# Two more output tiles by seven products behind an attention stage, and less plain work per run of it

## The chip, the cores and the metric

One core of a Trainium2 chip runs the kernel. TensorE multiplies, VectorE (DVE in the profile), ScalarE (ACT) and GpSimd (POOL) work on tiles, SyncE (SP) issues nearly all DMAs from one queue. The metric is the device time of one execution in microseconds (us). Before the change it is 987.44 us, the median of three runs (986.08 to 991.76).

## The reference, cut to what matters

One layer of neighbourhood attention over 2048 tokens (a grid of 32 rows and 64 columns), 1024 channels, 16 heads of 64 channels; all in float32.

```python
h = rmsnorm(x, g)
q, k, v, gate = split(h @ w_in, 4)                # 2048x1024 @ 1024x4096
# each query sees 8 rows x 16 columns of keys; rpb is a bias per head and offset
p = softmax(where(col_valid, q k^T / 8 + bias, -1e30))
x = x + ((p v) * silu(gate)) @ w_out              # 2048x1024 @ 1024x1024
return rmsnorm(x, norm_f)
```

## The kernel before, in words

A float32 product is taken as three TensorE matmuls: each operand is split into a high part (ScalarE, a copy to the fp32r type) and the rest (VectorE, a subtraction), and high x high, high x low and low x high are added up in PSUM. A pair of output tiles can be had in two ways. The plain way takes for each of four 128x512 quarters eight blocks of the inner dimension, 4 x 24 = 96 matmuls of 128x512. The other way is a scheme of seven products on sums and differences of the quarters (`order7`, `uses`), 7 x 12 = 84 matmuls, with more additions on VectorE and ScalarE.

Stage one and stage two compute the projections, mostly by seven products, and store q, k, v and the gate to DRAM. Six half projections of the last head pairs are left over: 288 plain matmuls. Then comes the attention stage, a loop of 32 *runs* over `order`. One run is one head pair p and one quarter T of the token rows. Run m does, in program order:

- `begin(m)` queues loads for the runs to come on SP (gate, bias tables `em`, q, k, v), each with a mark of TensorE that it must wait for (`not_until`);
- `feed` hands out plain products, some `amount[m]` of them, with `normalise` of the run before and splits of weights (`consume`, `split_rows`) between them;
- `turns(m-1)` transposes the attention weights of the run before (`ph`, 48 transposes) and ScalarE and VectorE copy them to SBUF (`pta`);
- `scores(2m)`, `scores(2m+1)`: 64 matmuls into `s`; VectorE adds the bias table, takes the extreme and writes `sums`; ScalarE takes the exponential into `x` with its sum; VectorE takes reciprocals; POOL normalises six of the eight tiles `x`, VectorE and ScalarE one each;
- `values(m-1)`: 36 matmuls into `o`, times the gate on VectorE, and a store to DRAM.

So plain products stand on TensorE between the value products and the next transposes, while the other engines turn scores into weights. The plain products are those 288, and then the first `PLAIN` output tiles (48 matmuls each, `outputs`). All other output tiles follow behind the attention stage by seven products (`rows_by_seven`, tiles in pairs from `PAIRS`). `amount` sets how many plain products each run gets: `dense` for the first runs, the rest spread evenly. In run 0 the loop also splits two input tiles (`consume(2, turn=True)`).

A bias table is of a kind: `top` for T = 0, `mid` for T = 1 and 2, `end` for T = 3. Run m brings the table of its kind; T = 0 also uses the `mid` of T = 1, T = 3 that of T = 2. Before, `order` takes T = 1 and 0 of all eight head pairs, then T = 2 and 3 of all; so each pair's `mid` is loaded twice.

Of the kernel before, what the change touches and what calls it, by code (L numbers as in the profile page):

```python
# [11 lines left out]
F32 = mybir.dt.float32  # L12
# [12 lines left out]
NP = H // 2  # L25
# [6 lines left out]
RES_BUFS, RES_EARLY = 3, 1  # L32
PLAIN = 4
BUSY = 2
# [28 lines left out]
def build(ctx, tc, x, xr, xt, wg, bias, w_out, n0, nf, out):  # L63
# [20 lines left out]
    raw = pool("raw", 6)  # L84
    kp = pool("kp", 1)
# [1112 lines left out]
    def projections():  # L1198
        for n, (kind, j, ph, c) in enumerate(halves):
            state["half"] = n  # L1200
            w = (KINDS[kind] + j, ph)
            for a in range(2):
                if n == len(halves) - 5 and a == 0:
                    for k in range(RES_EARLY):
                        load_res(*turns_[k])
                if n == len(halves) - 1:
                    if a == 0:
                        store(("ogl",), 20, lambda: load_og(0))
                        store(("ogl",), 38, lambda: load_og(1))
                    else:  # L1210
                        store(("og0",), 13, lambda: split_og(0))
# [22 lines left out]
    def load_k(p, T, part=None, at="values"):  # L1234
# [55 lines left out]

    def load_bias(p, T):
        fs = []
        kind = BRINGS[T]
        w = 2 * WIDE * TABLES[kind][2]
        EM[p, T // 2, kind] = []
        for quad in range(2):
            t = mp([128, 512], F32, "em")[:, :w]
            EM[p, T // 2, kind].append([t[:, :w // 2], t[:, w // 2:]])
            o = TABLE_AT[kind] + quad * w
# [34 lines left out]
    def scores(i, between=None):  # L1334
# [18 lines left out]
        for half, (u, n) in enumerate(HALF_ROWS[T]):  # L1353
            table = EM[p, T // 2, kinds_of[T][half]][quad]
            rows = [t[:, :24 * n].rearrange("p (r c) -> p r c", c=24) for t in sums[2 * half:2 * half + 2]]
# [124 lines left out]
    def add_rows(n, j, ps):  # L1480
        xr = RES.pop((n, j))
        state["event"] = clock[0]
        if n not in Y:
            Y[n] = [None, None], tiny.tile([128, 8], F32, name="st3")
        y, st = (raw if j and n < 1 else ev)([128, 512], F32, "y"), Y[n][1]
        Y[n][0][j] = y
# [88 lines left out]

    turns_ = [(0, 0), (1, 0), (2, 0), (0, 1), (1, 1), (2, 1), (3, 0), (3, 1)]
    place = {}
# [217 lines left out]
    cycles = len(order)  # L1795
    dense, end_of_it = 13.5, 24
    amount = [dense] * 25
    first = 16
# [3 lines left out]
    HALF_HEAD, HEAD = 2, 5  # L1802
    amount += [(96 * (12 - len(units_two)) + 48 * PLAIN - sum(amount) - first - end_of_it) / (cycles - 25)] * (cycles - 25) + [end_of_it - 6]
    fill = projections()
# [31 lines left out]
    def begin(m):  # L1836
# [118 lines left out]
```

## Time and profile before

| | us |
|---|---|
| median of 3 runs | 987.44 |
| the profiled execution | 987.61 |
| its span, first to last instruction | 985.8 |
| stages ahead of attention | 0 to 561.6 |
| attention, 32 runs | 561.6 to 865 |
| products behind attention | 865 to 979.5 |
| tail | 979.5 to 985.8 |

The granted clock of TensorE is 0.998 over the span. Busy times are those of the hardware profiler; matmuls are pipelined, so that a busy TensorE alone doesn't say how fast it goes, and the distance between starts is what counts.

### The profile page before, as it was taken

Reading aid. Unit: us, or ns where it says so; the run is one execution under the profiler, and the core shown is the slowest. Engines: PE = TensorE matmul, PEld = TensorE weight load, DVE = VectorE, ACT = ScalarE, POOL = GpSimd, SP = SyncE. Lnnn points to the kernel's source line nnn. Section 1 sums busy time; section 2 is a strip of 40 time slices with the busy share of each in tenths; the row PEclk is TensorE's granted clock in tenths of the full one; section 3 lists DMA queues with packets and bytes.
Section 4 is the critical chain, followed back from the end, with each engine's and each line's share of the span. In section 5 each row is a group of like instructions: output and inputs, shape, how many; then the busy total and the mean of one; then the engine's idle time right before and its main releaser. Section 6 shows DMA issues by size and latency. Waiting matters only on the chain.

```text
span 985.8 us, 22680 instructions
## 1 busy us (share of the span) xinstructions
PE 977.6 (99%) x8172; PEld 795.1 (81%) x8172; DVE 755.4 (77%) x1735; ACT 531.4 (54%) x1310; POOL 154.4 (16%) x378
## 2 busy tenths in 40 slices
PE   9999999999999999999999999999999999999997
PEld 6888888888888888888888777777777778788886
DVE  5899888988565876766776577677778888877866
ACT  7873245365535342333433377777777777653443
POOL 0000001222100000000001043333332333311110
PEclk9999999999999999999999999999999999999999
DMA  8943647777957846657555799888988988796854
GB/s 281 341 129 107 197 126 255 245 236 253 371 157 226 269 135 177 203 174 226 185 174 184 238 306 294 258 253 255 305 288 273 289 237 264 241 383 181 212 141 117
DMA packets 151617, 226.37 MB, mean 230 GB/s; under 512 B 13776, under 2 KB 67152, under 8 KB 151504
## 3 DMA queue, kind: packets, MB, share of 16 engines
q1 hardware_dynamic: 148480, 219.80, 70.6%
q0 software_dynamic: 2592, 4.72, 2.9%
q8 instruction: 65, 1.06, 0.4%
q14 instruction: 48, 0.39, 0.1%
q10 hardware_dynamic: 432, 0.40, 0.1%
HBM read 158.80 MB, written 66.06 MB: 228 GB/s over the span
## 4 chain that ended last, share of the span: by engine, by line
PE 98%; DMA 1%; SPq 0%; ACT 0%; issue 0%; DVE 0%
PE pp L447 41%; PE pv L613 13%; PE py L1725 12%; PE o L1423 8%; PE s L1347 6%; PE ph L1398 5%; PE pp L389 2%; PE pp L385 2%; PE pp L387 2%; PE pv L728 2%; PE po L1630 2%; PE po L1634 2%; PE po L1632 2%; DMA land<-in_xt_dram 1%; SPq L558 0%
## 5 line engine op out<-in xcount | busy, mean ns | idle before, releaser
L447 PE MATMUL pp<-h,f 128*128 128x512 f32 x576 | 185.3, 389 | 0.0
L447 PE MATMUL pp<-t,f 128*128 128x512 f32 x702 | 171.3, 389 | 0.0
L447 PEld LDWEIGHTS pp<-t,f 128*128 128x128 f32 x702 | 131.8, 188 | 27.4
L1366 ACT ACTIVATE x<-sums,st 128x264 f32<-128x264 f32 (+1 forms) x256 | 124.5, 488 | 29.9 <-DVE st L1358 29.9
L447 PEld LDWEIGHTS pp<-h,f 128*128 128x128 f32 x576 | 108.1, 188 | 22.6
L447 PE MATMUL pp<-l,f 128*128 128x512 f32 x288 | 112.0, 389 | 0.0
L1378 POOL TENSOR_SCALAR x<-x,st 128x264 f32<-128x264 f32 (+1 forms) x192 | 88.6, 477 | 130.1 <-DVE st L1373 106.0
L1358 DVE CUSTOM_DVE_ANT_0 sums<-s,em 128x253 f32<-128x253 f32 (+1 forms) x256 | 91.1, 401 | 5.8 <-ACT x L1366 1.5
L430 DVE TENSOR_TENSOR f<-raw,f 128x512 fp32r<-128x512 f32 x105 | 75.8, 727 | 19.3 <-ACT f L429 19.2
L1423 PEld LDWEIGHTS o<-pta,vt 120*64 120x64 f32 (+2 forms) x1152 | 70.0, 137 | 18.4 <-issue 11.7
L1423 PE MATMUL o<-pta,vt 120*64 120x192 f32 (+8 forms) x1152 | 84.1, 299 | 0.1
L429 ACT ACTIVATE f<-raw 128x512 fp32r<-128x512 f32 x105 | 63.5, 622 | 36.4 <-DVE raw L436 22.0
L1403 DVE COPY pta<-ph 120x512 f32<-120x512 f32 (+2 forms) x96 | 60.3, 682 | 14.8 <-PE ph L1398 14.5
L1405 ACT ACTIVATE pta<-ph 120x512 f32<-120x512 f32 (+2 forms) x96 | 50.3, 595 | 34.2 <-PE ph L1398 34.0
L447 PEld LDWEIGHTS pp<-l,f 128*128 128x128 f32 x288 | 54.1, 188 | 11.2
L1347 PE MATMUL s<-kt,q 64*32 64x253 f32 (+1 forms) x2048 | 59.3, 362 | 0.5 <-issue 0.5
L613 PE MATMUL pv<-wh,t 128*128 128x512 f32 x176 | 56.2, 389 | 0.0
L1725 PE MATMUL py<-woh,f 128*128 128x512 f32 x168 | 55.4, 390 | 0.0
L1398 PEld LDWEIGHTS ph<-ident,x 64*120 64x120 f32 (+2 forms) x1536 | 46.2, 128 | 11.3 <-issue 10.6
L468 POOL TENSOR_TENSOR tmp<-tmp,rb 128x512 f32<-128x512 f32 x18 | 28.5, 1582 | 157.8 <-DVE tmp L465 140.2
L447 PE MATMUL pp<-sixths,f 128*128 128x512 f32 x198 | 52.7, 389 | 0.0
L429 ACT ACTIVATE f<-s 128x512 fp32r<-128x512 f32 x42 | 26.2, 624 | 45.7 <-DVE s L436 39.8
(231 smaller groups left out, 1908.0 us busy)
## 6 DMA issues: line engine op xcount, KB each, us to landing
raw<-in_wg_dram SPq DMA_DIRECT2D x124, 256.0 KB, 5.0
row<-in_xr_dram SPq DMA_DIRECT2D x32, 256.0 KB, 5.1
vd<-v SPq DMA_DIRECT2D x32, 256.0 KB, 3.2
sgd<-sg SPq DMA_DIRECT2D x32, 256.0 KB, 3.3
q<-qd SPq DMA_DIRECT2D x32, 256.0 KB, 4.0
sgt<-sgd SPq DMA_DIRECT2D x32, 256.0 KB, 4.5
ogd<-og SPq DMA_DIRECT2D x32, 256.0 KB, 5.1
em<-in_bias_dram SPq DMA_DIRECT2D x32, 253.0 KB, 4.5
```

The source lines that it names most:

```text
L429: nc.scalar.activation(t[:, 0], src, AF.Copy)
L430: nc.vector.tensor_tensor(t[:, 1], src, t[:, 0].bitcast(F32), OP.subtract)
L447: nc.tensor.matmul(B[n, P], t[:, int(m == 2), c], x[k][int(m == 1)], start=P in (1, 6, 5) and k == 0 and m == 0, stop=k == 3 and m == 2, s ...
L613: nc.tensor.matmul(p, a[:, o], b, start=P in (1, 6, 5) and k == 0 and m == 0, stop=k == 3 and m == 2, skip_group_check=True)
L1347: product = nc.tensor.matmul(places[half, s][h * 32:h * 32 + 32], qt[a, g * 64 + half * 32:g * 64 + half * 32 + 32], kt[a, o:o + n * GW].r ...
L1358: nc.vector.tensor_tensor_reduce(rows[s][:, :, :WIDE], places[half, s].rearrange("p (r c) -> p r c", c=WIDE), table[s].rearrange("p (r c) ...
L1366: nc.scalar.activation(to, rows[s].rearrange("p r (b c) -> p b r c", b=3), AF.Exp, bias=st[:, o:o + 1], scale=-1.0, accum_out=st[:, 4 + o: ...
L1378: nc.gpsimd.tensor_scalar(t, t, f, 1.0, op0=OP.mult, op1=OP.mult)
L1398: one_turn = nc.tensor.transpose(ph[h][:k, o:o + 64], X[quad, half, s][q, at:at + k], ident[q, q])
L1403: nc.vector.tensor_copy(o, i_)
L1423: product = nc.tensor.matmul(o[s * 64:s * 64 + 64, g0 * 64:g1 * 64], vt[:k, strip, s * 64:s * 64 + 64], moving, start=strip == 0, stop=str ...
L1725: nc.tensor.matmul(B[m, P], t[:, a, c], b, start=P in (1, 6, 5) and k == 0 and i == 0, stop=k == 3 and i == 2, skip_group_check=True)
```

## The change

`PLAIN` goes from 4 to 2: two output tiles fewer stand in the attention stage as plain products (96 matmuls), and `PAIRS` has seven pairs instead of six (84 more matmuls behind it). `amount` is 9.7 products for the first 13 runs and the even rest after them, where it was 13.5. For the first three head pairs `order` now takes T = 1, 0, 2, 3 one after the other, and these four runs share one `mid` table of each quad; one of the next pair's two `mid` tables is loaded a run earlier. The two k buffers take turns by load and no longer by pair. Four output half tiles (`turns_`) are left in the stage instead of eight, all in the `ev` buffers, and three lags of their loads and splits are longer.

```diff
-PLAIN = 4
+PLAIN = 2
+SHARED = 3
...
-    order = [(p, T) for p in range(NP) for T in (1, 0)] + [(p, T) for p in range(NP - 2) for T in (2, 3)]
+    order = [(p, T) for p in range(SHARED) for T in (1, 0, 2, 3)]
+    order += [(p, T) for p in range(SHARED, NP) for T in (1, 0)] + [(p, T) for p in range(SHARED, NP - 2) for T in (2, 3)]
...
-                KT[p, T // 2] = (kp([128, 2048], F32, "kt") if p % 2 == 0 else mkp([128, 1536], F32, "kt"))[:, :1344]
+                KT[p, T // 2] = (mkp([128, 1536], F32, "kt") if len(KT) % 2 else kp([128, 2048], F32, "kt"))[:, :1344]
...
+    def table_at(p, T, kind):
+        return p, 0 if p < SHARED else T // 2, kind
+
-    def load_bias(p, T):
+    def load_bias(p, T, upto=2):
...
-        EM[p, T // 2, kind] = []
-        for quad in range(2):
+        got = EM.setdefault(table_at(p, T, kind), [])
+        for quad in range(len(got), upto):
...
-    turns_ = [(0, 0), (1, 0), (2, 0), (0, 1), (1, 1), (2, 1), (3, 0), (3, 1)]
+    turns_ = [(0, 0), (1, 0), (0, 1), (1, 1)]
...
-    dense, end_of_it = 13.5, 24
-    amount = [dense] * 25
+    dense, end_of_it = 9.7, 24
+    many = 13
+    amount = [dense] * many
...
+            if order[m][0] < SHARED and order[m][1] == 2:
+                fs += load_bias(*order[m + 2], 1)
```

What it moves is seen in the order of each engine's instructions. On TensorE, the plain products (`pp`) of run 4 up to its first transpose (`ph`); before, the last eleven of 13:

```order
L387 MATMUL pp<-l,w 128x512
L389 MATMUL pp<-h,w 128x512
L385 MATMUL pp<-h,w 128x512
L387 MATMUL pp<-l,w 128x512
L389 MATMUL pp<-h,w 128x512
L385 MATMUL pp<-h,w 128x512
L387 MATMUL pp<-l,w 128x512
L389 MATMUL pp<-h,w 128x512
L385 MATMUL pp<-h,w 128x512
L387 MATMUL pp<-l,w 128x512
L389 MATMUL pp<-h,w 128x512
L1398 MATMUL ph_6135<-ident,x_5191 120x64
```

and now all of them, from the last value product (`o`) on:

```order
L1428 MATMUL o<-pta,vt 64x128 x2
L388 MATMUL pp<-l,w 128x512
L390 MATMUL pp<-h,w 128x512
L386 MATMUL pp<-h,w 128x512
L388 MATMUL pp<-l,w 128x512
L390 MATMUL pp<-h,w 128x512
L386 MATMUL pp<-h,w 128x512
L388 MATMUL pp<-l,w 128x512
L1403 MATMUL ph_6093<-ident,x_5191 120x64
```

Seven products stand there where 13 stood. By run, from 0 to 31, they are now 39, 10, 9, 13, 7, 9, 10, 10, 12, 7, 10, 10, 11, 11, 11, 12, 10, 14, 8, 14, 8, 11, 11, 11, 11, 12, 11, 13, 10, 10, 14 and 15; before they were 47, 11, 13, 14, 13, 14, 13, 16, 11 and then 13 to 16.

On ScalarE, run 0 between the last exponential and the copies of the transposes; `h` are the two input tiles, `x_5207` the tile that it normalises, `w` weights, `k` a projection on its way out. Before:

```order
L1366 ACTIVATE x_5207,st<-sums,st 128x3x88
L545 ACTIVATE h<-raw 128x512 x2
L371 ACTIVATE k<-pp 128x512
L1380 ACTIVATE x_5207<-x_5207,st 128x3x88
L186 ACTIVATE w<-raw 128x512 x2
L371 ACTIVATE k<-pp 128x512
L1405 ACTIVATE pta<-ph_5388 120x2x4x64
```

Now:

```order
L1371 ACTIVATE x_5207,st<-sums,st 128x3x88
L546 ACTIVATE h<-raw 128x512 x2
L1385 ACTIVATE x_5207<-x_5207,st 128x3x88
L187 ACTIVATE w<-raw 128x512
L372 ACTIVATE k<-pp 128x512
L187 ACTIVATE w<-raw 128x512
L1410 ACTIVATE pta<-ph_5370 120x2x4x64
```

The first `k` has left the run, the second stands between the two weights; VectorE's order in run 0 is the same in both kernels.

On VectorE, run 27 from the gate product (`og`) to the first copy. Before, with an output half tile's addition (`y<-po,xr`) and two scalings:

```order
L1429 TENSOR_TENSOR og<-o,sgt 128x512
L1373 RECIPROCAL st<-st 128x2
L1504 TENSOR_TENSOR y<-po,xr 128x512
L1373 RECIPROCAL st<-st 128x2
L1382 TENSOR_SCALAR x_5205<-x_5205,st 128x3x64
L1546 SCALAR_TENSOR_TENSOR y<-y,st_9124,acc_175 128x512
L1546 SCALAR_TENSOR_TENSOR y<-y,st_9124,acc_176 128x512
L1403 COPY pta<-ph_10469 96x2x4x64
```

Now, with two splits of w_out (`wol`):

```order
L1434 TENSOR_TENSOR og<-o,sgt 128x512
L1378 RECIPROCAL st<-st 128x2 x2
L1387 TENSOR_SCALAR x_5205<-x_5205,st 128x3x64
L193 TENSOR_TENSOR wol<-raw,woh 128x512 x2
L1408 COPY pta<-ph_10308 96x2x4x64
```

The splits of w_out stood in runs 11 to 15 and 19 to 24 before, and stand in runs 16 to 19 and 25 to 29 now; the splits of an output tile's rows (`gl`, two operations each) stood in runs 17, 19, 20 and 25, and stand in 24 and 25.

More of the change, by code (lines that the diff above doesn't have):

```diff
@@ L1207, in projections @@
                     if a == 0:
-                        store(("ogl",), 20, lambda: load_og(0))
-                        store(("ogl",), 38, lambda: load_og(1))
+                        store(("ogl",), 29, lambda: load_og(0))
+                        store(("ogl",), 42, lambda: load_og(1))
                     else:
-                        store(("og0",), 13, lambda: split_og(0))
+                        store(("og0",), 20, lambda: split_og(0))
                 consume(1)
@@ L1353, in scores @@
         for half, (u, n) in enumerate(HALF_ROWS[T]):
-            table = EM[p, T // 2, kinds_of[T][half]][quad]
+            table = EM[table_at(p, T, kinds_of[T][half])][quad]
             rows = [t[:, :24 * n].rearrange("p (r c) -> p r c", c=24) for t in sums[2 * half:2 * half + 2]]
@@ L1484, in add_rows @@
             Y[n] = [None, None], tiny.tile([128, 8], F32, name="st3")
-        y, st = (raw if j and n < 1 else ev)([128, 512], F32, "y"), Y[n][1]
+        y, st = ev([128, 512], F32, "y"), Y[n][1]
         Y[n][0][j] = y
@@ L1802, in build @@
     HALF_HEAD, HEAD = 2, 5
-    amount += [(96 * (12 - len(units_two)) + 48 * PLAIN - sum(amount) - first - end_of_it) / (cycles - 25)] * (cycles - 25) + [end_of_it - 6]
+    amount += [(96 * (12 - len(units_two)) + 48 * PLAIN - sum(amount) - first - end_of_it) / (cycles - many)] * (cycles - many) + [end_of_it - 6]
     fill = projections()
```

2 lines of the change are left out of this document (1 added, 1 removed).

## The prediction, as put on record before the result

> **What bounds the kernel now.** I read the profile page's busy line and its chain first, to see which engine sets the end; then the busy times by stage; then the chain within the attention stage, run by run (run m is pass m of the attention loop, counted from 0).
>
> ```profile
> span 985.8 us, 22680 instructions
> ...
> PE 977.6 (99%) x8172; PEld 795.1 (81%) x8172; DVE 755.4 (77%) x1735; ACT 531.4 (54%) x1310; POOL 154.4 (16%) x378
> ...
> PE 98%; DMA 1%; SPq 0%; ACT 0%; issue 0%; DVE 0%
> ```
>
> TensorE (PE) is 98% of the chain that ended last. So time is saved only by taking matmuls out, and lost only where another engine makes TensorE wait. The stages, one row each (run 0; runs 1 to 12; 13 to 18; 19 to 28; 29 to 31; the products behind attention and the tail):
>
> ```profile
> 561.60:576.40 14.80, 14.80 (x161) 11.14 (x160) 10.37 (x32) 10.14 (x28) 4.53 (x11) 1.00 0.91 298
> 576.40:686.30 109.90, 109.39 (x1938) 86.55 (x1935) 82.83 (x313) 81.67 (x259) 40.99 (x145) 1.00 0.89 267
> 686.30:741.00 54.70, 54.70 (x973) 43.48 (x969) 43.66 (x160) 41.85 (x132) 20.10 (x68) 1.00 0.95 300
> 741.00:833.00 92.00, 91.95 (x1621) 72.91 (x1617) 78.14 (x288) 70.61 (x225) 30.43 (x85) 1.00 0.87 261
> 833.00:865.00 32.00, 32.00 (x534) 25.53 (x531) 27.54 (x95) 22.01 (x71) 9.14 (x22) 1.00 0.80 257
> 865.00:985.80 120.80, 114.50 (x504) 94.40 (x504) 88.32 (x173) 49.94 (x119) 15.89 (x18) 0.98 0.70 205
> ```
>
> After the stage's length come PE, PEld, DVE (VectorE), ACT (ScalarE) and POOL, then the granted clock, the DMA share and GB/s. TensorE is full everywhere; VectorE is at 75% in runs 1 to 12 and 85% in runs 19 to 28 (78.14 of 92.00), with the DMAs at 0.80 to 0.95. The attention stage is where the change takes TensorE work away, so there the other engines' room decides.
>
> **The change, part by part.** First the matmuls. The chain in order of time gives their price:
>
> ```profile
> 695.46 1.87 PE s L1347 x64
> ...
> 699.88 0.43 PE pp L389
> 700.31 0.24 PE pp L385
> ...
> 702.86 0.23 PE pp L389
> 703.09 1.56 PE ph L1398 x48
> 704.65 1.64 PE s L1347 x64
> ...
> 864.96 114.56 PE py L1725 x504
> ```
>
> Behind attention a 128x512 product costs 114.56 / 504 = 0.227 us. In run 14 the 13 plain products between the value products (o) and the transposes (ph) take 703.09 - 699.88 = 3.21 us, one slow first one and then 0.23 each. The change removes two output tiles of 2 x 24 plain products: 96 x 0.23 = 22.1 us. It adds one pair by seven products, 7 x 12 = 84: 84 x 0.227 = 19.1 us. **Term 1: -3.0 us** (at 0.227 for both, -2.7).
>
> Next the cover. A run keeps 9.7 products where it had 13.5, later about 11. Scores go out at the start of a run; VectorE reduces them, ScalarE takes the exponentials, POOL, ScalarE and VectorE normalise, and only then may the transposes come. Run 14 again, in the timeline:
>
> ```profile
> 694.64 1.88 DVE L1403 COPY pta<-ph 88x512 f32<-88x512 f32 x3 [0.20 <-PE ph L1398]
> ...
> 696.57 0.42 DVE L1358 CUSTOM_DVE_ANT_0 sums<-s,em 128x253 f32<-128x253 f32 x1
> ...
> 697.09 0.52 ACT L1366 ACTIVATE x<-sums,st 128x264 f32<-128x264 f32 x1 [0.92 <-DVE st L1358]
> ...
> 701.42 0.52 ACT L1380 ACTIVATE x<-x,st 128x264 f32<-128x264 f32 x1 [0.23 <-DVE st L1373]
> ...
> 701.50 0.47 DVE L1382 TENSOR_SCALAR x<-x,st 128x264 f32<-128x264 f32 x1
> ```
>
> The last normalised tile is ready at 701.97; the transposes start at 703.09 and need it with the 13th of 48, at 703.09 + 13 x 1.56 / 48 = 703.5. Slack: 1.5 us, or 6.5 products. The order of the changed kernel leaves 7 products in runs 4 and 9, 8 in 18 and 20, 9 to 15 elsewhere. Even the shortest, 6 x 0.23 = 1.4 us less than run 14, still fits, by 0.1 us. So the nominal run is covered to its end, with nothing over for anything late. Three places have something late.
>
> *Run 0.* VectorE and ScalarE also normalise and split input tiles there:
>
> ```profile
> 569.08 0.73 DVE L541 SCALAR_TENSOR_TENSOR raw<-raw,g,rb 128x512 f32<-128x512 f32 x1
> ...
> 572.96 0.69 DVE L546 TENSOR_TENSOR l<-raw,h 128x512 fp32r<-128x512 f32 x1 [0.76 <-ACT h L545]
> 573.57 0.22 DVE L1373 RECIPROCAL st<-st 128x2 f32<-128x2 f32 x2
> ...
> 573.89 1.05 POOL L1378 TENSOR_SCALAR x<-x,st 128x264 f32<-128x264 f32 x2 [2.89 <-DVE st L1373]
> ```
>
> and in the chain the transposes that follow:
>
> ```profile
> 574.90 1.56 PE ph L1398 x48
> ```
>
> The reciprocals that POOL needs stand behind those input tiles on VectorE, until 573.79; POOL is done at 574.94. The 11th transpose, which reads POOL's last tile, came at 574.90 + 10 x 1.56 / 48 = 575.22: 0.3 us of slack. VectorE's order up to there is unchanged and its waits are for ScalarE, not for TensorE, so POOL will still end near 574.9. But 8 products go (47 to 39), 1.8 us. **Term 2: 1.8 - 0.3 = +1.5 us**, bounds 0 (the VectorE chain moves forward too) and 1.8.
>
> That wait holds all of TensorE. [...]
>
> *Runs 1 to 6.* Each splits one weight on VectorE between the last normalisation and the copies, as before, after a late start out of run 0. VectorE needs 701.97 - 696.57 = 5.4 us from first reduction to last normalisation and 1.88 for the copies, 7.3 together; every second run has four short reductions, 0.07 us cheaper each, so 7.15 is the mean. A split costs 0.65 and waits for ScalarE:
>
> ```profile
> L1358 DVE CUSTOM_DVE_ANT_0 sums<-s,em 128x253 f32<-128x253 f32 x192 | 73.1, 418 | 5.1 <-ACT x L1366 1.5 <-PE s L1347 0.4
> ...
> L1358 DVE CUSTOM_DVE_ANT_0 sums<-s,em 128x184 f32<-128x184 f32 x64 | 20.4, 347 | 0.7
> ```
>
> ```profile
> 693.15 1.29 DVE L192 TENSOR_TENSOR wol<-raw,woh 128x512 fp32r<-128x512 f32 x2 [0.63 <-ACT woh L191]
> ```
>
> With 0.63 for that wait a run needs 7.15 + 0.65 + 0.63 = 8.4 us of VectorE's time. On TensorE a run is 704.65 - 695.46 = 9.19 us at 13 products, so 6.2 us fixed; six runs with 58 products are 6 x 6.2 + 58 x 0.23 = 50.5 us against 50.4. Balanced: the lag out of run 0 doesn't heal. (Runs 16 to 19, with two w_out splits each and 46 products, come to 36.3 against 35.4; the next paragraph shows that this sum reads high by as much, so nothing is taken for them.) **Term 3: +0.5 us**, bounds 0 and 1.2.
>
> *Runs 25 to 29.* By the changed order the w_out splits, one output tile's split and two additions fall together: 12 VectorE operations in five runs with 56 products. VectorE: 5 x 7.15 + 12 x 0.65 + 5 x 0.63 = 46.7 us; TensorE: 5 x 6.2 + 56 x 0.23 = 43.9. Before, runs 19 to 25 had 18 such operations, between these two starts of scores:
>
> ```profile
> 741.09 1.64 PE s L1347 x64
> ...
> 805.53 1.87 PE s L1347 x64
> ```
>
> The same sum there gives 7 x 7.15 + 18 x 0.65 + 7 x 0.63 = 66.2 us where 64.4 were measured, so it reads 1.3 us too high per five runs. Left: 2.8 - 1.3 = 1.5, of which the transposes' own slack at 10 to 13 products (0.8 to 1.5 us) takes some once. **Term 4: +1.0 us**, bounds 0 and 2.8.
>
> *Table sharing.* Six loads fall away:
>
> ```profile
> em<-in_bias_dram SPq DMA_DIRECT2D x32, 253.0 KB, 4.5
> ```
>
> That is 1.5 MB of the stage's 82 MB (lengths times GB/s above). A load takes 4.5 us and is asked for a run or more ahead, so none is waited for now and none saves time; it offsets what the shorter runs ask for. Were that cover gone, the price is rival D. *Behind attention* VectorE has the roots and scaling of two tiles to do at once, about 2.9 us more (1.7 for the eight small operations from 867.64, 1.42 for two scalings, less 0.2 of overlap), ahead of row sums that had slack:
>
> ```profile
> 867.64 0.21 DVE L1531 TENSOR_SCALAR st<-st 128x1 f32<-128x1 f32 x1
> ...
> 869.35 1.42 DVE L1546 SCALAR_TENSOR_TENSOR y<-y,st,acc 128x512 f32<-128x512 f32 x2
> ...
> 873.40 0.69 DVE L1698 TENSOR_TENSOR s<-raw 128x512 f32<-128x512 f32 x1 [2.63 <-DMA raw<-ogd]
> ...
> 875.59 0.69 DVE L1692 TENSOR_TENSOR f<-s,f 128x512 fp32r<-128x512 f32 x1
> ```
>
> VectorE waited 2.63 us there for a DMA, and the form made at 875.59 is used by the seventh group, at 864.96 + 72 x 0.227 = 881.3. Nothing is paid.
>
> Sum: -3.0 + 1.5 + 0.5 + 1.0 = 0.0 us on the profiled 987.61 (span 985.8 and 1.8 around it), which lies 0.2 over the median of 987.44. **Forecast: 987.4 us, no change.** Bounds: -3.0 gives 984.4, -3.0 + 1.8 + 1.2 + 2.8 = +2.8 gives 990.2. What a measurement can tell from no change is about 0.5%, 4.9 us; no sum of these terms reaches it.
>
> **The rivals.** *B, the cover holds everywhere:* terms 3 and 4 vanish, term 2 partly: 984.4 to 986. For it: VectorE waits 14.5 us in the stage for transposes, time that shorter runs take first (the row under C); against it: run 0's 0.3 us. Price taken: 985.
>
> *C, VectorE becomes the bound of the whole stage (slower):*
>
> ```profile
> DVE pta L1403 <- PE ph L1398: 14.5, 21, 2.6
> ```
>
> The stage's five rows sum to 303.4 us with 242.5 busy on VectorE, 61 idle. About 11 us go with the two tiles (4 additions at 0.69, 4 scalings at 0.71, 4 splits at 0.65, the roots). TensorE's stage becomes 303 - 22 = 281. If VectorE's idle time shrinks only by half of what it waits for transposes (the row above), it needs 231.5 + 61 - 7 = 285.5, +4; if not at all, +11. With -3.0 and run 0's 1.5 that makes 990 to 997; I price it 994. It decides once the average run needs over 8.5 us of VectorE; runs 1 to 6 stand at 8.4.
>
> *D, loads or code come late.* The stage asks for some 4 MB less (tables 1.5, two tiles' attention rows 1.0, their x rows 1.0), 79 MB in 281 us, 280 GB/s against 272: hardly more. But run 10 shows a stall that no semaphore explains:
>
> ```profile
> 657.90 1.85 PE s L1347 x61
> 659.75 0.51 issue
> 660.27 0.61 PE s L1347 x3
> ```
>
> The block of scores took 660.88 - 657.90 = 3.0 us instead of 1.9, with the DMAs at 0.89. One such in every fourth run is 8 us: 993. Against it: one in 32 now.
>
> [...]
>
> **How the numbers follow.** Forecast 0.52, B 0.26, C 0.14, D 0.08. The forecast and most of B lie within 0.5% (982.5 to 992.4); a few hundredths of B could go below, if a stall like run 10's falls away with it; C and D are mostly above, a quarter of them within. Faster 0.04, same 0.78, slower 0.18. The range takes the bounds, 984.4 to 990.2, and a little of C: 984.2 to 991.5.
>
> **What would show it.** Term 1: 588 products at 0.227 behind attention (133.6 us), and TensorE still over 98% of the chain. Term 2: transposes of run 0 waiting for POOL over 1 us. Terms 3 and 4: waits of transposes for VectorE's or ScalarE's normalisation in runs 1 to 6 and 25 to 29, none in 7 to 15. I am wrong if run 0 doesn't wait, if waits stand in every run (C), or if "issue" grows in the chain (D).

## The result, and the profile after

The changed kernel takes 994.44 us, the median of 10 runs (991.53 to 997.21), beside 987.2 us before (10 runs, 986.08 to 991.76): a ratio of 1.007, with a 95% interval of 1.005 to 1.0089. It is slower, and above the range of the forecast. Its times fall in two groups, five about 992.4 and five about 996.5. In later rounds the same kernel had 990.75 to 997.13; over all its 18 timed runs the median is 993.0, with 987.3 for the kernel before in the same rounds. So the change costs some 5.5 to 7 us, 0.5 to 0.7 per cent.

The page of the profiled execution (992.85 us, of the lower group) has the same busy line as before; of the chain's shares TensorE loses two points:

```profile
span 991.1 us, 22671 instructions
...
PE 978.6 (99%) x8160; PEld 794.2 (80%) x8160; DVE 754.5 (76%) x1734; ACT 534.3 (54%) x1317; POOL 157.0 (16%) x381
...
PE 96%; ACT 1%; DVE 1%; DMA 1%; issue 0%; SPq 0%; POOL 0%; ACTq 0%
```

A busy TensorE of 99% says little: a product behind attention is recorded with 390 ns (the page's mean for L1730), while the next one starts 227 ns later, so that a short wait between two leaves no idle time. The stages say more (run 0; runs 1 to 12; 13 to 18; 19 to 28; 29 to 31; behind attention):

```profile
561.75:575.96 14.21, 13.34 (x152) 9.80 (x151) 10.04 (x32) 9.38 (x26) 4.50 (x11) 1.00 0.93 281
575.96:677.99 102.03, 100.75 (x1892) 79.11 (x1889) 78.85 (x308) 79.07 (x254) 38.56 (x122) 1.00 0.90 270
677.99:729.90 51.91, 51.66 (x960) 40.79 (x958) 41.87 (x158) 41.07 (x130) 20.54 (x72) 1.00 0.88 267
729.90:819.90 90.00, 88.34 (x1612) 69.16 (x1606) 72.33 (x268) 69.96 (x221) 32.13 (x101) 1.00 0.92 280
819.90:851.10 31.20, 31.12 (x524) 24.53 (x522) 24.42 (x85) 22.95 (x73) 8.63 (x22) 1.00 0.77 258
851.10:991.10 140.00, 133.72 (x590) 110.28 (x588) 104.78 (x210) 56.82 (x136) 18.51 (x21) 0.99 0.67 193
```

From the first score to the first product behind attention it is 289.4 us, where it was 303.3: 13.9 less. Of the 96 products that are gone 94 stood in this stretch and two just ahead of it; 94 are worth 21.6 us, so 7.7 were lost here. Behind attention 19.0 us are added (139.94 for 120.95), as forecast. All that is missing was lost inside the attention stage.

To see where, I take each run's length (first score to first score) less 0.23 us per plain product and less 6.19 us in even, 5.84 in odd runs, which are the lengths of runs without a wait (even runs mostly have the longer scores; runs 0, 30 and 31 have lengths of their own). What is left over is called *excess* below. Before, all runs together have 1.5 us of it, of which run 10 has 1.08 (the stall the prediction showed). After, it is 9.2 us, 7.7 more, and in few runs: 1.36 in run 0; 1.88 in runs 1 to 5; 0.60 in run 6 and 0.47 in run 7; 0.60 in run 18; 1.62 in run 24; 1.31 and 0.27 in runs 26 and 27; 1.05 in run 29, of which 0.32 were there before. Runs 8 to 17, with 7 to 14 products each, have 0.14 together.

What TensorE waited for in the stage, in the view of waits (us in total, times, longest):

```profile
PE o L1428 <- issue: 1.8, 3, 0.8
PE ph L1403 <- POOL x L1383: 0.9, 2, 0.7
PE po L1635 <- ACT gh L1476: 0.6, 1, 0.6
PE pp L390 <- issue: 0.3, 1, 0.3
PE po L1637 <- DVE gl L1477: 0.2, 1, 0.2
```

Run 0, in the chain in order of time: VectorE's reciprocals end at 573.55 and POOL's two tiles at 574.70, while the transposes before them have run out.

```profile
573.40 0.15 DVE st L1378 x2
...
573.64 1.06 POOL x L1383 x2
...
574.75 1.38 PE ph L1403 x38
```

Run 24, which the prediction did not look at: the first output tile is used here, and its split (gh on ScalarE, gl on VectorE) stands in program order just ahead of its use and of the normalisation. So not only the first output product waits; the reciprocals and the last `x` come behind gl, and the transposes with them.

```profile
779.00 0.53 ACT gh L1476
...
779.55 1.29 DVE gl L1477 x2
780.85 0.15 DVE st L1378 x2
...
781.08 0.53 ACT x L1385
...
781.65 0.48 POOL x L1383
...
782.19 1.32 PE ph L1403 x38
```

Runs 28 and 29, in the timeline of VectorE: two w_out splits that wait for ScalarE, an addition, and only then the copies of run 28's transposes, which TensorE had begun at 818.08; the first reduction of run 29 starts 2.3 us behind the scores of 819.64, where runs that wait for nothing mostly have 1.1 to 1.3.

```profile
818.38 1.29 DVE L193 TENSOR_TENSOR wol<-raw,woh 128x512 fp32r<-128x512 f32 x2 [0.50 <-ACT woh L192]
819.59 0.68 DVE L1509 TENSOR_TENSOR y<-po,xr 128x512 f32<-128x512 f32 x1
820.19 1.87 DVE L1408 COPY pta<-ph 120x512 f32<-120x512 f32 x3
821.98 0.41 DVE L1363 CUSTOM_DVE_ANT_0 sums<-s,em 128x253 f32<-128x253 f32 x1
```

And run 3, in the chain: a stall in the middle of the value products, which no semaphore explains. There are four such in this profile, 2.2 us idle in all, where the profile before has one, of 0.51 us.

```profile
594.68 0.58 PE o L1428 x7
595.26 0.81 issue
596.07 2.23 PE o L1428 x29
```

### The profile page after: what moved, and what is told of

The parts are those of the page before. It is cut to its first block, busy times and chain, and to the rows that moved or that the text cites. A ratio compares the mean times of both kernels' runs of the same rounds, so it can differ in the third digit from the quotient of the medians.

```text
span 991.1 us, 22671 instructions
## 1 busy us (share of the span) xinstructions
PE 978.6 (99%) x8160; PEld 794.2 (80%) x8160; DVE 754.5 (76%) x1734; ACT 534.3 (54%) x1317; POOL 157.0 (16%) x381
## 3 DMA queue, kind: packets, MB, share of 16 engines
q8 instruction: 64, 1.05, 0.4%
## 4 chain that ended last, share of the span: by engine, by line
PE 96%; ACT 1%; DVE 1%; DMA 1%; issue 0%; SPq 0%; POOL 0%; ACTq 0%
PE pp L448 40%; PE py L1730 13%; PE pv L614 13%; PE o L1428 8%; PE s L1352 6%; PE ph L1403 5%; PE pp L390 2%; PE pp L386 2%; PE pp L388 2%; PE pv L729 2%; PE po L1637 1%; PE po L1639 1%; PE po L1635 1%; ACT x L1371 1%; DMA land<-in_xt_dram 0%
## 5 line engine op out<-in xcount | busy, mean ns | idle before, releaser
L1730 PE MATMUL py<-woh,f 128*128 128x512 f32 x196 | 64.7, 390 | 0.0
L1403 PE MATMUL ph<-ident,x 64*120 64x64 f32 (+2 forms) x1536 | 52.1, 220 | 0.9 <-POOL x L1383 0.9
```

The costliest lines, as they stand in the source:

```text
L1403: one_turn = nc.tensor.transpose(ph[h][:k, o:o + 64], X[quad, half, s][q, at:at + k], ident[q, q])
L1730: nc.tensor.matmul(B[m, P], t[:, a, c], b, start=P in (1, 6, 5) and k == 0 and i == 0, stop=k == 3 and i == 2, skip_group_check=True)
```

## The experiments

Two theories stand against each other. *Waits*: the loss is a sum of waits with causes that the program's order makes (run 0, runs 1 to 5, run 24, runs 26 to 29), the same in every execution. *Code*: TensorE's instructions, which are loaded while it runs (64 fetches, 1.05 MB, on queue q8 of the page), come late, and this makes the rest and the upper group of times. Each kernel was timed beside the kernel before in the same rounds, whose median was 987.25 to 987.8 us throughout.

| run | edit to | median us | ratio to before | 95% interval |
|---|---|---|---|---|
| c1_again | change, as it is | 992.82 | 1.0055 | 1.0035 to 1.0076 |
| c1_run0 | change | 996.21 | 1.0094 | 1.0069 to 1.0119 |
| c1_split | change | 992.76 | 1.0056 | 1.0037 to 1.0076 |
| c1_noshare | change | 993.22 | 1.0057 | 1.0041 to 1.0074 |
| c2_run0 | change | 994.35 | 1.0068 | 1.0052 to 1.0083 |
| c2_pool | change | 991.38 | 1.0033 | 1.0020 to 1.0046 |
| c2_light | change | 992.49 | 1.0054 | 1.0033 to 1.0075 |
| c2_before_light | before | 986.88 | 0.9994 | 0.9985 to 1.0003 |
| c3_split | change | 990.83 | 1.0041 | 1.0022 to 1.0059 |
| c3_mend | change | 989.88 | 1.0033 | 1.0020 to 1.0045 |
| c4_relief | change | 989.94 | 1.0026 | 1.0017 to 1.0035 |
| c4_spread | change | 997.31 | 1.0092 | 1.0076 to 1.0109 |
| c4_front | change | 991.03 | 1.0031 | 1.0017 to 1.0045 |
| c5_before_relief | before | 986.38 | 0.9985 | 0.9976 to 0.9995 |
| c5_front_relief | change | 987.21 | 0.9996 | 0.9987 to 1.0004 |

**One suspect at a time.** The first four: the change again; run 0 with 46 products; the first attention output split eight products earlier; the tables not shared.

> The changed kernel once more, beside the others of this call. Theory W (single waits): TensorE work in attention is 22 us less and behind it 19 us more, and some 8 us of waits stand in single runs: about 1.3 us in run 0 (normalised tiles late), 1.7 us in run 24 (first output tile's rows split too late for its product), 1 us in run 29 (VectorE behind), and four stretches of 0.5 to 1.1 us in which TensorE waits for nothing that the profile shows. Theory V (VectorE bounds the whole stage): waits in most runs. Both expect 992 to 997 us; W expects the transposes to come late in no more than 8 of 32 runs.

> Five products go back into run 0 and two into run 1, taken evenly from the later runs; nothing is left out. W: run 0's wait of 1.3 us goes, and the time falls by 1 to 1.5 us against the changed kernel. V: the runs that lose products lose as much as run 0 gains, so the time stays within 0.5 us.

```diff
-    amount[0] -= first / 2
-    amount[1] += first
+    amount[0] += 5 - first / 2
+    amount[1] += first + 2
```

> The split of the first output tile's rows is due 8 products earlier (lag 12 for 20), so that it stands in run 23 and no longer in run 24. W: the 1.7 us that the first output product waits in run 24 go, if the rows have landed by then; if they haven't, ScalarE waits for them ahead of its copies in run 23 and about 1 us stays. V: no change beyond 0.5 us.

```diff
-                        store(("og0",), 20, lambda: split_og(0))
+                        store(("og0",), 12, lambda: split_og(0))
```

> The changed kernel with the order and tables of before (SHARED 0): six more table loads, 1.5 MB. If the DMAs' load makes code and tiles come late (theory D), it is slower by 1 to 4 us, with more stretches in which TensorE waits for nothing shown. If it doesn't, the time is within 0.7 us of the changed kernel.

```diff
-SHARED = 3
+SHARED = 0
```

The sharing of tables and the order of the runs with it make no difference that shows (993.22 beside 992.82). With 46 products run 0's excess fell from 1.36 to 0.13 us, so that wait is the one named. But the time rose by 3.4 us. Some 0.4 to 0.7 us more of excess came up in each of runs 13, 14, 16, 17, 22 and 25, which more than makes up for what run 0 gave back. By the shifted spread the splits of w_out and of the first attention output stand a run earlier; what each of those six runs waits for was not followed up. The rest is an upper group at 998 to 1000, three of the six times, which was not profiled here; such times are taken up below. The split in run 23 took run 24's 1.62 us away, and put 0.70 into run 23, where it stood ahead of the normalisation again. Of the 0.9 us left the median shows nothing (992.76), and the profile has 3.8 us in run 3 alone, with a stall of 1.90 us without a cause.

**The same suspects without shifting the products.** Two normalised tiles of run 0 from POOL to VectorE and ScalarE; and the low parts of the weights on POOL instead of VectorE.

> In the run 0 alone, two of the six tiles that POOL normalises go to VectorE and ScalarE; the spread of the products is not touched (unlike in the run with 46 products). In the changed kernel the transposes of run 0 wait 1.37 us for POOL's last two tiles. If that wait is a cost of its own: run 0 takes 13.0 to 13.3 us instead of 14.31, and the time falls by 1.0 to 1.4 us to about 991.6. If what one wait gives back is eaten by the next (what the run with 46 products looked like): no change from 992.8, and the excess of run 1 rises by the same 1.3 us.

```diff
-            if quad == 0 or half == 0:
+            if quad == 0 or half == 0 and i > 1:
```

> The low parts of the weights that are split in the attention stage from run 1 on (6 of the last projections, 16 of w_out) are subtracted on POOL instead of VectorE (1.63 us each there in stage two, 0.69 us on VectorE). If the waits of runs 1 to 6 (1.0 us in all) and of runs 26, 27 and 29 (0.8, 0.3 to 0.6 and 1.05 us) are a late VectorE: they vanish, and the time falls by 2.5 to 3 us to about 990. If they are loads or code that come late: they stay where they are, and the time stays within 0.5 us of 992.8. If POOL becomes the late engine in its turn, transposes wait for its tiles in the same runs and the time rises.

```diff
             nc.scalar.activation(h, t, AF.Copy)
-            nc.vector.tensor_tensor(l, t, h.bitcast(F32), OP.subtract)
+            (nc.gpsimd if runs[0] else nc.vector).tensor_tensor(l, t, h.bitcast(F32), OP.subtract)
...
             nc.scalar.activation(h, t, AF.Copy)
-            nc.vector.tensor_tensor(l, t, h.bitcast(F32), OP.subtract)
+            nc.gpsimd.tensor_tensor(l, t, h.bitcast(F32), OP.subtract)
```

Run 0 fell to 1.10 us only, and run 1 rose from 0.29 to 0.98: with a tile more, ScalarE came late with its copies (the last of them at 576.11 us; the scores of run 1 waited 0.4 us for it). The wait was handed on. The median, 994.35, is above both expectations, since four of the six times are 994.2 to 997.0; the profile, at 992.43, doesn't show why. POOL, on the other hand, does the subtractions where it has nothing to do, though it takes 1.29 us for one (VectorE 0.69, the mean of the same 16 in the change):

```profile
L193 POOL TENSOR_TENSOR wol<-raw,woh 128x512 fp32r<-128x512 f32 x16 | 20.3, 1290 | 6.6 <-ACT woh L192 6.6
```

The excess of runs 1 and 2 went from 0.54 to 0.03, that of run 26 from 0.81 to nothing, of run 27 from 0.6 to 0.16, of run 29 from 1.03 to 0.33, which is what run 29 has before the change. That of run 4, with 7 products, did not fall (0.42; 0.31 in c1_again). So term 4 of the prediction and the part of term 3 in runs 1 and 2 are VectorE's, as it said; the median fell by 1.4 us, where 2.5 to 3 were expected.

**Are the stalls a matter of load?** One q tile and one gate tile for the whole stage, 62 loads (16 of 81 MB) less, in both kernels.

> The changed kernel with one q tile and one gate tile loaded for the whole attention stage, 62 loads of 256 KB less (16 of 81 MB there); so queries and gates of all runs but the first are wrong, and that part of the computation is left out. If TensorE's stalls without a cause (0.4 to 4.5 us in the five profiles of the change so far) come from instruction fetches that queue behind loads: they go to under 0.5 us, and the time falls by 1.5 to 3 us to about 990.5. If they don't depend on the load: they stay, and the time stays within 0.5 us. In both cases the waits of runs 0, 24, 26 and 29 stay.

> The kernel before with the same 62 loads less (queries and gates of all runs but the first are wrong, that part of the computation is left out). Its profile shows 1.1 to 1.5 us of such stalls. If they come from late instruction fetches behind loads: 986.0, and the distance to the changed kernel with the same edit is the waits alone less the work saved, about +4.5 us (6.5 of waits, 1.0 of other stages within the error, less 3.0). If they don't depend on the load: 987.4, and the distance stays at 5.5 to 7 us.

```diff
         def queries():
+            if QT:
+                QT[p, T] = QT[order[0]]
+                return
             QT[p, T] = qp([128, 512], F32, "q")
...
     def load_sg(p, T):
+        if one_gate:
+            SG[p, T] = one_gate[0]
+            return
         SG[p, T] = sp([128, 512], F32, "sgt")
```

Neither profile has a stall of over 0.2 us without a cause any more, but two of the change's six times are still 995.5 and 996.9, and its median stayed at 992.49. Undecided: around run 3 the DMA engines were still full (0.98 to 1.11 busy from 586 to 596 us).

**What helped, put together, and an execution of the upper group.**

> The changed kernel with the low parts of weights on POOL from run 1 on, and the split of the first attention output (gh, gl) five products earlier, behind the normalisation of run 23 instead of ahead of that of run 24. In the run with POOL alone, run 24 still has 1.62 us over the others and run 0 1.36 us. If each named wait is a cost by itself: run 24 falls to the others, nothing new in run 23, and the time falls by a further 1.0 to 1.6 us, to about 990. If split and normalisation trade one wait for another (as in the run with the split eight products earlier, where 0.7 us came up in run 23): 991.4, no change.

> The same with the split three products earlier, and six products more in run 0, taken evenly from the later runs (0.3 of a product each). If the waits named so far (run 0: 1.36, runs 1 to 6: 1.0, run 24: 1.62, runs 26 to 29: 2.5) are all that the changed kernel loses for certain: the sum over the runs falls from 7.0 us to under 1.5 us beside what is stalled for code, attention takes about 282 us, and the time is 987 to 988.5, no change against the kernel before or just above it. If a wait given back in one place comes up in the next (the run with 46 products): over 990.5.

Both have the low parts on POOL, as above. The first edit below is that of c3_split, the second that of c3_mend.

```diff
-                        store(("og0",), 20, lambda: split_og(0))
+                        store(("og0",), 15, lambda: split_og(0))
```

```diff
-                        store(("og0",), 20, lambda: split_og(0))
+                        store(("og0",), 17, lambda: split_og(0))
...
-    amount[0] -= first / 2
+    amount[0] += 6 - first / 2
```

Behind the normalisation of run 23 the split costs nothing there, and run 24's excess is gone (-0.03). The median fell by 0.6 us, to 990.83, where 1.0 to 1.6 were expected; its times reach from 986.93 to 997.6. The second kernel's median is 989.88, not 987 to 988.5: in its profile the runs 0, 2, 13, 22, 24 and 25 keep 0.4 to 0.9 us each. This profile was by chance an execution of 1001.32 us, and shows what such a long one has in it. In the chain:

```profile
593.43 1.64 PE s L1352 x64
595.07 0.36 PE o L1428 x2
595.43 3.19 issue
598.62 4.25 PE o L1428 x32
```

The value products take 4.25 us after the stall, where 36 of them take 2.55 without one. The granted clock, in the column ahead of the DMA share, tells why:

```profile
593.00:595.00 2.00, 2.00 (x81) 1.45 (x75) 2.00 (x6) 1.16 (x4) 0.53 (x5) 1.00 1.10 292
595.00:598.60 3.60, 0.43 (x10) 0.19 (x2) 2.30 (x16) 3.60 (x15) 1.75 (x4) 1.00 1.05 324
598.60:602.00 3.40, 3.38 (x27) 3.38 (x29) 0.00 (x0) 0.20 (x2) 0.00 (x0) 0.50 0.37 130
602.00:604.00 2.00, 2.00 (x16) 1.63 (x13) 1.05 (x4) 0.19 (x1) 0.23 (x1) 1.00 0.75 182
```

After 3.19 us of idleness TensorE has half its clock for 3.4 us, and so loses some 2 us more. Run 6 has the same again (2.56 idle, excess 5.46). The other profile of the upper group, 997.51 us with the split moved, has one such place (2.89 idle, excess 4.83 in run 3).

> The changed kernel once more, for its profile alone: its times fall in two groups, about 992 and 996.5 us, and the profiles so far are of the lower one. If the upper group has one stall for code of some 2 us with TensorE at half its clock for 3.4 us behind it (seen once, in the run with the split eight products earlier: 1.90 us without a cause, then clock 0.50, 3.8 us in all): a profile of that group shows such a place. If it has late loads: TensorE waits for a DMA in it. If all waits are a little longer: the excess is spread over the runs.

> As the other repetition of the changed kernel: a profile at about 992 us shows waits of 6.5 us with known causes and under 2 us without one; a profile at about 996.5 us shows by its excess, run by run, where the 4 us more come from: one long stall with half the clock behind it, late loads, or all waits a little longer.

Two more profiles of the unchanged change came at 994.03 and 991.73: excess 10.5 and 8.9 us, of which the stalls without a cause are 3.4 and 1.0 us; no wait for a load in either. The causes named above stand in both with the same sizes (run 0 1.36, run 24 1.63, run 29 1.05). Neither is of the upper group, so that half the clock behind a stall also makes the upper group of the change itself is not shown; the three profiles of over 997 us, all of edited kernels, have it.

Where do these stalls stand? I counted TensorE's instructions in 19 profiles of this study: a weight load and a matmul each, and the semaphore waits between. All 44 stalls of over 0.2 us inside a block of value products, scores or plain products without a named cause begin within two instructions of one place, 193 more than a multiple of 256. The page has the fetches as a queue of their own, 64 of 16 KB in the program:

```profile
q8 instruction: 64, 1.05, 0.4%
```

64 fetches for some 16600 instructions is one for every 256. And the time of the fetch gives the stall. In run 3 of the 1001.32 us profile the 256 instructions up to that place took 6.7 us; their successor's fetch started 7.5 us after their beginning, and the first new instruction followed 2.40 us after that start: 7.5 + 2.4 - 6.7 = 3.2, for a stall of 3.19. In the changed kernel's own profile, run 3, it is 4.2 + 2.6 - 6.1 = 0.7 for 0.81; in the kernel before, run 10, 5.3 + 2.4 - 7.2 = 0.5 for 0.51. So in these three the fetch started later than some 2.4 us ahead of its place: 1.9 us ahead of it in two, 0.8 behind it in the longest stall. Where 256 instructions fall on one run's transposes, scores and value products, they take 4.2 to 6.8 us; some 12 of 40 stretches are under 6.8 us before, 14 of 40 after.

**What makes a fetch late, and where the cover should stand.**

> The changed kernel with one q tile, one gate tile and one v tile for the whole attention stage, 93 loads and about 29 of 81 MB less there (the output is that of a wrong attention; that part of the computation is left out). In all profiles so far a stall for code goes with an instruction fetch that starts late in its run: in run 3 a fetch 0.2 us ahead of the run's start leaves an excess of 0.3 us, one 2.9 us behind it 5.3 us. With 16 MB less the DMA engines were still full around run 3 (1.00 busy), and two of six times were over 995. If the fetch is late because the DMA engines are full: at 29 MB less they aren't, the upper group of times disappears (none above 993.5), stalls without a cause are under 0.5 us, and the median falls to about 990.5. If the fetch is late for another reason: an upper group as before, with the fetch of run 3 as late as 1 to 3 us in some profile.

Beside one q and one gate tile, as above:

```diff
+        if one_v:
+            VT[p, T] = one_v[0]
+            return
         t = vp([128, 1024], F32, "vt")
```

> The changed kernel with its plain products spread otherwise, and the order of the runs as before (its tables are then not shared; that alone made no difference): 12.5 instead of 9.7 products in each of the first eight runs, and about 9.8 instead of 10.8 in the later ones. The early runs are those with w splits on VectorE, with full DMA engines and with the longest stalls for code; runs 8 to 21 of the change waited for nothing at 7 to 12 products. If the place of the cover decides: runs 0 to 7 lose under 0.5 us instead of 3 to 8 (excess of the runs 0 to 7 in the profile of the change: 4.3 us), the upper group of times disappears, and the time is 988.5 to 990. If only the total of cover counts: the later runs lose what the early ones gain, and the time stays at 992 to 994.

> The same spread (12.5 products in each of the first eight runs) with the low parts of weights on POOL and the split of the first attention output behind the normalisation of run 22: all that helped so far together. If the losses add up as told (run 0 and runs 1 to 7 about 4 us, run 24 1.6, runs 26 to 29 2.5): under 1.5 us are left of the 9 us of excess, and the time is 985.5 to 987.5, at or below the kernel before, which would show that the products moved are worth their 3 us where nothing waits. If late runs with 7 products and a split now wait instead: 988 to 990.

```diff
-SHARED = 3
+SHARED = 0
...
-    dense, end_of_it = 9.7, 24
-    many = 13
+    dense, end_of_it = 12.5, 24
+    many = 8
```

In c4_front also the low parts on POOL, as above, and

```diff
-                        store(("og0",), 20, lambda: split_og(0))
+                        store(("og0",), 17, lambda: split_og(0))
```

With 29 MB less the upper group is gone: ten times from 989.16 to 992.19, nine of them under 990.3. The fetches start 0.6 us after the beginning of their 256 instructions (median), where it is 1.1 with 16 MB less, 1.7 in the change and 1.9 in the kernel before. One stall of 0.79 us is left (under 0.5 was expected), in the value products of run 3, at the same place of the count and 2.4 us after its fetch started; the view gives it to VectorE's `st`, which has nothing to do with them and came last before it. The waits with a cause stand as they were:

```profile
PE ph L1416 <- POOL x L1396: 0.9, 2, 0.7
PE s L1365 <- DVE y L1522: 0.8, 1, 0.8
PE o L1441 <- DVE st L1376: 0.8, 1, 0.8
PE po L1648 <- ACT gh L1489: 0.6, 1, 0.6
```

So the fetches came earlier with the DMA engines 0.58 busy than with 0.89, as in the change. The spread alone made it worse, 997.31, against what both theories said: its runs 2 and 3 have 14 and 11 products and still 3.7 and 2.1 us of excess, from a fetch each that came late, one of them with half the clock behind it. And most of its runs from 14 on, with 7 to 13 products, now have 0.3 to 1.2 us each. The 14 products of run 2 didn't shield it from a late fetch. With all that helped, 991.03 us, above both expectations: the lowest time, 987.55, is at the kernel before. The profile has 7.7 us of excess left and not under 1.5, of which late fetches make 3.8 (2.1 idle in run 3, 0.7 in run 10).

**The two shares.** The 93 loads left out in the kernel before as well, and in the best version.

> The kernel before with the same 93 loads left out (one q, one gate and one v tile; the attention that it computes is wrong, and that part is left out). Beside the changed kernel with the same edit (989.94) it gives what the change costs where instruction fetches come in time. If the change costs 3 us by its waits (6.1 of waits less 3.0) and the rest by late fetches: 986 to 987, 3 to 4 us below 989.94. If the kernel before loses as much to late fetches as the change: 983.5 to 985, and the whole distance of 5.5 to 7 us is waits.

> The kernel with all that helped (12.5 products in each of the first eight runs, low parts on POOL, the split behind the normalisation of run 22) and the same 93 loads left out (the attention that it computes is wrong, and that part is left out). Its profile without this edit has 3.9 us of waits with a cause and 3.8 us of stalls for code. If the move of 84 for 96 products is worth its 3 us and the waits add up: 986.5 to 987.5 with these waits left, so 0 to 1 us above the kernel before with the same edit, against 3 to 4 us for the changed kernel. If the waits with a cause grow or shrink with the loads: outside of this.

The kernel before falls by 1.0 us to 986.38, so late fetches cost it about 1.0. The change falls by 3.1 to 4.5 us to 989.94 (from 993.0 over all its runs, or 994.44 at first). Nearly without late fetches the change still costs 989.94 - 986.38 = 3.6 us. By the two profiles the excess is 7.7 us, 0.8 of it a late fetch, against -0.2: 7.1 us of waits less the 3.0 us of saved products is 4.1. With the late fetch it is 4.9. The two spans differ by 3.3 only, since attention began at 560.5 us in one and at 562.5 in the other; 0.5 of that are the two products ahead of it, which are in the 3.0 already, and the rest is of the size by which this start varies between profiles of changed kernels (560.5 to 562.3). The best version is at 987.21, +0.8, inside the 0 to 1 that was expected; its excess is 3.9 us, 4.1 above -0.2, less 3.0 is +1.1. The only wait of TensorE left there in the view of waits:

```profile
PE ph L1416 <- ACT x L1398: 0.2, 1, 0.2
```

The rest of its excess lies inside blocks of transposes (1.95 us in run 14, where 1.55 is usual) and of scores (2.17 in run 27 for 1.64), in gaps too short for the view; which engine they wait for is not shown.

## Why the prediction was wrong

**The chain as the bound** was right: TensorE is 96% of the chain that ended last, and what the change cost is nearly all time in which TensorE stood or, behind some long stalls of the edited kernels, had half its clock.

**Term 1 (-3.0) held.** 588 products behind attention in 133.63 us, 0.227 each, as written down beforehand:

```profile
851.20 133.63 PE py L1730 x588
```

The best version shows that the 22.1 us for 96 plain products are real as well: where little waits, the balance comes out near -3.0 plus the waits.

**Term 2 (+1.5, run 0) held**: 1.36 us, with POOL's last two tiles as the cause, in every profile of the change. POOL ended at 574.70, where 574.9 was forecast. The term takes it that nothing else fills the wait, which no row of before showed; this profile does, since from 573.60 to 574.75 TensorE ran no more than two transposes.

**Term 3 (+0.5, runs 1 to 6) was undersized**: about 1.0 us, inside its bounds. In runs 1 and 2 it is VectorE's, since it went away when POOL took the splits; in run 4 it stayed.

**Term 4 (+1.0, runs 25 to 29) was undersized**: some 2.2 us (run 26 0.8, run 27 0.6, run 29 0.7 more than before), inside its bounds of 0 to 2.8.

Both sums share a wrong step: they take 6.2 us for TensorE's fixed part in every run, from run 14. That is an even run, whose scores take 1.87 us; in the next, by the prediction's own chain, they take 1.64, and the fixed part of such runs is 5.84. With three of each, runs 1 to 6 come to 49.4 us and not 50.5, so VectorE with its 50.4 is 1.0 short; with three long and two short, runs 25 to 29 come to 43.1 and not 43.9, so it is 3.6 short, or 2.3 without the 1.3 by which that sum reads high. That is close to what was measured, though term 3 took no such correction. What a sum can't tell is where the wait falls. At the end of run 26 the first scores of run 27 waited for the addition `y`, which reads the output tile in PSUM and stands on VectorE behind two w_out splits:

```profile
PE s L1352 <- DVE y L1509: 0.8, 1, 0.8
```

(This row is from the repetition of the change; in the first profile a late fetch in the same run hid it.)

**"Three places have something late" was the first step that failed.** Run 24 is a fourth, at 1.6 us, and runs 19 to 22 add 0.2 to 0.5. The change moved the split's lag from 13 to 20, so that one output tile's split stands in run 24 and one in run 25. The prediction counted that of run 25 among its twelve operations and that of run 24 nowhere. By the order it stood ahead of both its first use and the run's normalisation. An edit to a lag should have been followed to the instructions that it puts next to each other.

**Rival D, put at nothing in the sum, was the second.** "One such in every fourth run is 8 us" has the places about right (runs 3, 6 or 7, 10 or 11, 18 and 26 over the four profiles of the change), but only one to four of them stalled in a profile. It was given a chance of 0.08, because the kernel before showed "one in 32" and the stage asks for hardly more bytes. The rate of bytes did not grow, 272 GB/s in both; but before, too, the fetches came in time by a narrow margin (four of 40 started no more than 2.5 us ahead of their place), with the DMA engines just as full (0.89 in both). Late fetches cost about 1.0 us before and 3.1 to 4.5 after, some 2 to 3.5 us more. That half the clock followed some stalls (3.4 us of it behind the one of 3.19) was no part of the prediction at all.

The bounds of the sum, up to +2.8, took zero for D and for run 24. With 1.6 for run 24 and 2 to 3.5 for D the terms as measured give -3.0 + 1.4 + 1.0 + 2.2 + 1.6 + 0.5 + 2 to 3.5 = +5.7 to +7.2, beside 5.5 to 7 measured. The last term is itself a difference of such times and proves nothing by fitting; the waits do stand by themselves, 6.7 us by their sizes and 3.6 + 3.0 = 6.6 by the runs with 93 loads less.

**Rival C fell**: runs 8 to 17 wait for nothing. VectorE got rid of more work than C assumed, too: it is busy for 227.5 us in the stage, where C reckoned with 231.5. But that 7 products still cover a run is shown for run 9 alone, a run with the short scores; run 4 has 7 too, and its wait stayed when POOL took its split. B fell with run 0.

**Occupancy or bytes, and the clock.** At 0.89 busy and 272 GB/s fetches came late. At 0.58 and 172 GB/s only one stall was left; both fell together there, so the runs don't separate the share of time in which the DMA engines are busy from the bytes that they move. Half the clock lasted 3.4 us in the rows above. How long TensorE must idle for it is not shown: stalls of 1.69 and 1.90 us were followed by half the clock in two profiles (c4_spread, c1_split), those of 2.13 and 1.72 in two others (c4_front, c3_split) were not. Nor is the fall tied to the stall's end: in one profile (c3_mend, run 6) it came 1.1 us ahead of it, in another (c4_spread, run 2) 0.6 us behind it.

## What to carry to other kernels

When cover is taken from a stage, list what stands ahead of each consumer in program order, run by run; a sum of busy times says that the work fits, but not that it is there in time, and an operation put just ahead of its use (the split in run 24) cost nearly its whole length, 1.6 of 1.8 us. Put such work behind the operations that release the bottleneck engine, and on an engine that is idle then, even a slower one (here a subtraction took 1.29 us on POOL against 0.69 on VectorE, and the median fell by 1.4). TensorE, with some 16600 instructions in 991 us, had 64 fetches of code here beside its data; with the DMA engines 0.89 busy in the stage, the stalls without a cause summed to 0.5, 2.2, 3.4 and 1.0 us in four profiles of the same kernel, so look at several executions before pricing one at its size in one.

## What the runs showed of the hardware

- TensorE's instructions were fetched by DMA during the run, 16 KB for 256 instructions, beside the data. In the stalls the next instruction ran 2.2 to 2.8 us after its fetch started (once 3.2). With the DMA engines at 0.85 to 0.91 busy the fetch started 1.5 to 2.2 us after the beginning of its stretch as a median, and up to 9.8 us in the places that stalled; at 0.74 busy (the two runs with 16 MB less) 1.0 and 1.1 us, at 0.58 to 0.61 busy (the three with 29 MB less) 0.6 to 0.8 us.
- Five of the eleven stalls over 1.4 us, of 1.69, 1.90, 2.56, 2.89 and 3.19 us, were followed by half the clock, for 3.4 us in four and 6.8 us in the one of 2.56; behind the one of 3.19 it added some 2 us. The stalls under 1.6 us kept the full clock.
- Moved to POOL, a 128x512 subtraction took 1.29 us instead of VectorE's 0.69, and no new wait of TensorE for POOL shows in the view of waits.

What stays open: why the fetch of run 3 waits 4 us in one execution and 7.5 in the next at the same load, and when TensorE asks for it. With 93 loads less it started at 592.4 us, 4.2 after its stretch began, though the DMA engines were only some 0.6 busy from 582.75 to 590 us and 0.5 from there to 597.25, where the change has 0.91 to 1.07 from 585 to 597; so full engines alone don't explain that one. Whether a program of the same work whose 256-instruction stretches end elsewhere would escape is open too; the other spreads of products moved them by the way (c4_spread, c4_front), and both still stalled.
